# Attention products of an encoder step regrouped into fewer tiled stretches, with the chunk mask carried as contraction rows

## The chip, the core and the metric

The kernel runs on one core of a Trainium2 chip. TensorE (PE in the profile) multiplies, and its weight loads are listed apart as PEld; VectorE (DVE), ScalarE (ACT) and GpSimd (POOL) work on the results, and SyncE (SP) issues the transfers. The metric is the device time of one execution in microseconds (us), less is better.

## The reference

One step of a two-layer streaming encoder: 512 prompt frames of one new stream (positions 0 to 511) and 16 new frames of each of 8 running streams with 256 cached positions. Layer 0 mixes with forgetting attention (FoX, 16 heads of 64), layer 1 with latent attention (MLA, 16 heads of 64 + 32 rotary dimensions, mask by chunks of 64 frames); each is followed by cross attention over 256 memory rows (4 heads of 256) and a SwiGLU block of width 2816.

```
# fox
s = einsum('bqhd,bkhd->bhqk', q, k) * FOX_SCALE + cum_q - cum_k
p = softmax(where(k_pos <= q_pos, s, -inf)); o = einsum('bhqk,bkhd->bqhd', p, v)
o = (o * sigmoid(gate)) @ w_out
# mla
s = (einsum('bqhn,bkhn->bhqk', qn, k_nope) + einsum('bqhr,bkr->bhqk', qr, kr_all)) * MLA_SCALE
p = softmax(where(k_pos // 64 <= q_pos // 64, s, -inf)); o = einsum('bhqk,bkhd->bqhd', p, v)
# each layer
x = x + mixer(rmsnorm(x)); x = x + cross_attn(rmsnorm(x), mem_k, mem_v); x = x + swiglu(rmsnorm(x))
```

## The kernel before

The 512 prompt frames and the 128 frames of the running streams are five tiles of 128 rows. All stages follow one another on one core: FoX, cross attention 0, SwiGLU 0, MLA, cross attention 1, SwiGLU 1. Weights and activations are kept as two rounded parts (`hi`, `lo`), and a product is three passes of matmuls (`mm3`, `PASSES`, helper line L212; the big products go through `gemm`, L198). A product of plain float32 operands is recorded as two matmuls for each one that the program issues.

In the attention stages `merge` spreads three lists of steps evenly over each other: the prompt's attention for one pair of heads (or one head), the running streams' attention, and a list of big products for other heads (the `fill`). A scheduler then lays the instructions of each engine out in one fixed order, and may pull single instructions ahead of others that it expects to wait. TensorE works through that order.

Most matmuls use TensorE's whole array of 128 rows by 128 columns. Some address a part of it, because an operand has fewer rows or the result goes to a part of PSUM's 128 partitions. This text calls such a matmul *tiled*, and an unbroken series of matmuls of one tiling a *run*:

- FoX scores of the prompt (`scores`, L212): 64 contraction rows, head 0 of the pair in rows 0 to 63, head 1 in 64 to 127. Three passes for head 0 stand ahead of three for head 1, for each of four query tiles with 512, 384, 256 and 128 keys.
- FoX and MLA values of the prompt (`values`, L614 and L1587): 64 result columns for each of the two heads, once for each query tile.
- Running streams in FoX (L662, L687) and in cross attention (`scores` L903, `values` L928): four streams in four column strips of 32. In cross attention the two heads of a pair are two steps, each with keys or values loaded anew (`vr`, two buffers).
- MLA's chunk mask (L1561): a product of one row, `mrow` (-1e30 for the first 64 queries of a tile, else 0) times `mcol` (ones), added to the last 64 keys of every score tile behind its three passes of 96 rows.
- MLA running streams, rotary part of the scores (L1497): 32 rows (`KR` times `QR`), behind two products of 128 rows (L1495).

Of the kernel before, what the change touches and what calls it, by code (L numbers as in the profile page):

```python
# [18 lines left out]
P = 128  # L19
D = 1024  # L20
KD = D // P
NP = 512
# [33 lines left out]
C_END = 784  # L56


def const_table():
# [17 lines left out]
    return c  # L77


@with_exitstack  # L80
def fox_mla_kernel(ctx: ExitStack, tc: tile.TileContext, I, O):
# [22 lines left out]
    mrow = const.tile([1, P], BF16, name="mrow")  # L104
    G.memset(mrow, 0.0)
    G.memset(mrow[:, 0:64], NEG)
    mcol = const.tile([1, 64], BF16, name="mcol")
    G.memset(mcol, 1.0)

# [77 lines left out]
    def gemm(ops, n, done, parts=1):  # L187
        """One PSUM accumulation as a list of steps; ops() is asked for when the first step runs."""
# [56 lines left out]
    class Act:  # L245
        """A transposed activation in two tiles of four row blocks each."""
# [36 lines left out]
    def out_norm(out_tile, g_row, cls=None):  # L283
        """Runs the last output projection of a phase tile by tile, each tile's norm behind it."""
# [86 lines left out]
    # ---------------------------------------------------------------- FOX  # L371
    def fox_phase():
# [8 lines left out]
        with ExitStack() as st:  # L381
# [13 lines left out]
            def pt_tile():  # L395
                return fp.tile([P, NP], F32, tag="PT", name="PT", bufs=3)
# [164 lines left out]
            def prompt_list(pr):  # L561
# [10 lines left out]
                def scores(qt):  # L572
                    n = P * (qt + 1)
                    qs = slice(qt * P, (qt + 1) * P)
                    kT, qT = ks[pr][0], qs_[pr][0]
                    d["pw"] = []
                    for hh in range(2):
                        h = 2 * pr + hh
                        rs = slice(64 * hh, 64 * hh + 64)
                        pw = pw_tile()  # L580
                        G.tensor_scalar(pw[:, 0:n], d["ck"][hh][:, 0:n], -1.0, cq[:, qt, h:h + 1], ALU.mult, ALU.add)
                        G.affine_select(pw[:, n - P:n], pw[:, n - P:n], pattern=[[-1, P]], compare_op=ALU.is_ge,
                                        fill=NEG, base=0, channel_multiplier=1)
                        sp = psum_s()
                        mm3(sp[:, 0:n], [q[rs, qs] for q in qT], [k[rs, 0:n] for k in kT])
                        nm = small.tile([P, 1], F32, tag="nm", name="nm")
                        V.tensor_tensor_reduce(out=pw[:, 0:n], in0=sp[:, 0:n], in1=pw[:, 0:n], scale=-1.0,
                                               scalar=3.0e38, op0=ALU.add, op1=ALU.min, accum_out=nm)
                        ss = small.tile([P, 1], F32, tag="ssum", name="ssum")
                        A.activation(pw[:, 0:n], pw[:, 0:n], AF.Exp, scale=-1.0, bias=nm, accum_out=ss)  # L590
                        softmax_tail(pw, ss, n)
                        d["pw"].append(pw)

                def trans(qt):
                    n = P * (qt + 1)
                    d["PT"] = []
                    for hh in range(2):
                        pt = psum_t()
                        for kt in range(qt + 1):
                            T.transpose(out=pt[:, kt * P:(kt + 1) * P], in_=d["pw"][hh][:, kt * P:(kt + 1) * P],  # L600
                                        identity=ident)
                        PTt = pt_tile()
                        if hh == 0:
# [3 lines left out]
                        d["PT"].append(PTt)  # L607

                def values(qt):
                    qs = slice(qt * P, (qt + 1) * P)  # L610
                    op = psum_o()
                    for kt in range(qt + 1):
                        for hh in range(2):
                            T.matmul(op[64 * hh:64 * hh + 64, 0:P],  # L614
                                     lhsT=vs[g][:, kt, j * P + 64 * hh:j * P + 64 * hh + 64],
                                     rhs=d["PT"][hh][:, kt * P:(kt + 1) * P], start=(kt == 0), stop=(kt == qt))
                    V.tensor_tensor(sg[pr][:, qs], op[:, 0:P], sg[pr][:, qs], ALU.mult)

                L = [load]
                for qt in reversed(range(TT - 1)):  # L620
                    L += [lambda qt=qt: scores(qt), lambda qt=qt: trans(qt), lambda qt=qt: values(qt)]
                return L
# [149 lines left out]
    # ---------------------------------------------------------------- cross attention  # L772
    def cross_phase(l, nx, rest):
# [3 lines left out]
        with tc.tile_pool(name=f"x{l}", bufs=2, reuse_waits="tile") as xp:  # L777
# [99 lines left out]
            def sample_list(pr, bq):  # L877
# [3 lines left out]
                def keys(hh, b):  # L881
                    hc = slice((2 * pr + hh) * XD, (2 * pr + hh + 1) * XD)
                    if b % 2 == 0:
                        d["KT"][b // 2] = xp.tile([P, 2, 2, NMEM], F32, tag="KT", name="KT", bufs=2)
# [8 lines left out]
                    if b % 2 == 0:  # L893
                        V.tensor_copy(d["KT"][b // 2][:, 0], src)
                    else:
                        A.copy(d["KT"][b // 2][:, 1], src)

                def scores(hh):
                    if hh == 0:
                        d["sp"] = psum_s()  # L900
                    for dt in range(2):
                        for b in range(4):
                            T.matmul(d["sp"][32 * b:32 * b + 32, 0:NMEM], lhsT=Q[:, 2 * hh + dt, 4 * bq + b, :],  # L903
                                     rhs=d["KT"][b // 2][:, b % 2, dt, :], start=(hh == 0 and dt == 0),
                                     stop=(hh == 1 and dt == 1), tile_position=(0, 32 * b))
                    if hh == 1:
                        d["pw"] = xp.tile([P, NMEM], F32, tag="pws", name="pws", bufs=2)
                        softmax(d["pw"], d["sp"])
# [8 lines left out]
                def values(hh):  # L917
                    if hh == 0:
                        d["op"] = psum_o()
                    hc = slice((2 * pr + hh) * XD, (2 * pr + hh + 1) * XD)  # L920
                    vr = []
                    for b2 in range(2):
                        v = xp.tile([P, 4, XD], F32, tag="vr", name="vr", bufs=2)
                        S.dma_start(v, mv[:, 8 * bq + 4 * b2:8 * bq + 4 * b2 + 4, hc])
                        vr.append(v)
                    for mt in range(2):
                        for b in range(4):
# [770 lines left out]
```

## Time and profile before

| | |
|---|---|
| median of 3 runs | 2170.16 us (2169.56 to 2170.47) |
| span of the profiled execution, first to last instruction | 2169.7 us |
| TensorE matmul busy | 2116.0 us, 98% of the span |
| TensorE weight load busy | 1862.4 us, 86% |
| VectorE, ScalarE, GpSimd busy | 65%, 42%, 8% |
| granted TensorE clock, mean | 0.997 of full speed (2.4 GHz) |
| FoX attention 70 to 512 us; cross attention 0 577 to 710; MLA attention 1262 to 1515; cross attention 1 1580 to 1735 | of the span |

The profiled execution's own time is its span; no other figure of it is listed. Matmuls overlap, and a matmul's recorded duration reaches beyond the start of the next one, so the busy share says only that the engine hardly stood idle. What a matmul costs is read from the distance between starts.

### The profile page before, as it was taken

Reading aid. Unit: us, or ns where it says so; the run is one execution under the profiler, and the core shown is the slowest. Engines: PE = TensorE matmul, PEld = TensorE weight load, DVE = VectorE, ACT = ScalarE, POOL = GpSimd, SP = SyncE. Lnnn points to the kernel's source line nnn. Section 1 sums busy time; section 2 is a strip of 40 time slices with the busy share of each in tenths; the row PEclk is TensorE's granted clock in tenths of the full one; section 3 lists DMA queues with packets and bytes.
Section 4 is the critical chain, followed back from the end, with each engine's and each line's share of the span. In section 5 each row is a group of like instructions: output and inputs, shape, how many; then the busy total and the mean of one; then the engine's idle time right before and its main releaser. Section 6 shows DMA issues by size and latency. Waiting matters only on the chain. (4 is left out here: it accounts for less than half of the span.)

```text
span 2169.7 us, 36108 instructions
## 1 busy us (share of the span) xinstructions
PE 2116.0 (98%) x14253; PEld 1862.4 (86%) x14253; DVE 1404.2 (65%) x2719; ACT 904.0 (42%) x1809; POOL 178.7 (8%) x354
## 2 busy tenths in 40 slices
PE   7999999999999999999999999999999999999998
PEld 7888888888977799999999877777886799999997
DVE  5455555655446796687676566667545796786685
ACT  4444434554433453343334454544433443343342
POOL 1222121120000000000000200100100000000000
PEclk9999999999999999999999999999999999999999
DMA  8353443576354322222221320112435322322221
GB/s 235 112 145 107 127 124 116 178 231 211 108 178 143 117 78 79 87 88 78 78 78 53 109 72 26 51 40 60 154 129 190 94 84 78 98 75 82 78 88 59
DMA packets 279273, 234.34 MB, mean 108 GB/s; under 512 B 15664, under 2 KB 255920, under 8 KB 279104
## 3 DMA queue, kind: packets, MB, share of 16 engines
q1 hardware_dynamic: 279104, 232.03, 34.9%
q8 instruction: 113, 1.85, 0.4%
q14 instruction: 56, 0.46, 0.1%
HBM read 214.79 MB, written 17.21 MB: 107 GB/s over the span
## 5 line engine op out<-in xcount | busy, mean ns | idle before, releaser
L198 PE MATMUL mm<-hT,whi 128*128 128x320 f32 x1744 | 296.3, 314 | 3.3 <-ACT hT L216 3.3
L198 PEld LDWEIGHTS mm<-hT,whi 128*128 128x128 f32 x1744 | 261.1, 188 | 16.0 <-issue 9.8
L312 DVE TENSOR_TENSOR X<-mm,X 128x512 f32<-128x512 f32 x270 | 183.2, 687 | 127.5 <-PE mm L198 125.6
L145 DVE TENSOR_TENSOR wlo<-raw,whi 128x1024 fp32r<-128x1024 f32 (+4 forms) x145 | 169.7, 1175 | 105.8 <-ACT whi L144 69.8
L144 ACT CAST whi<-raw 128x1024 fp32r<-128x1024 f32 (+4 forms) x145 | 144.0, 1002 | 122.7 <-PE mm L198 75.6
L198 PE MATMUL mm<-whi,oT 128*128 128x512 f32 x544 | 185.2, 413 | 2.4 <-DVE X L312 2.1
L1069 ACT CAST whi<-tw 128x512 fp32r<-128x512 f32 (+1 forms) x120 | 91.9, 766 | 213.8 <-PE mm L198 127.5
L198 PE MATMUL mm<-whi,aT 128*128 128x512 f32 x560 | 173.0, 390 | 0.3 <-ACT aT L1034 0.3
L198 PE MATMUL mm<-hT,wlo 128*128 128x320 f32 x872 | 157.4, 313 | 0.0
L198 PEld LDWEIGHTS mm<-hT,wlo 128*128 128x128 f32 x872 | 133.7, 188 | 3.6 <-issue 3.5
L198 PE MATMUL mm<-whi,hT 128*128 128x256 f32 (+2 forms) x800 | 126.8, 297 | 1.9 <-ACT hT L216 1.0
L198 PE MATMUL mm<-s,whi 128*128 128x320 f32 x768 | 128.2, 309 | 0.0
L226 POOL TENSOR_SCALAR rstd<-ss 128x1 f32<-128x1 f32 x49 | 16.7, 340 | 1306.2 <-ACT hn L224 1302.1
L198 PEld LDWEIGHTS mm<-whi,aT 128*128 128x128 f32 x560 | 104.4, 188 | 22.5 <-ACT aT L1034 1.2
L198 PEld LDWEIGHTS mm<-whi,oT 128*128 128x128 f32 x544 | 98.0, 190 | 26.1 <-issue 5.7
L198 PEld LDWEIGHTS mm<-s,whi 128*128 128x128 f32 x768 | 116.6, 188 | 0.0
L198 PEld LDWEIGHTS mm<-whi,hT 128*128 128x128 f32 x800 | 109.5, 192 | 7.8 <-issue 3.2
L1070 DVE TENSOR_TENSOR wlo<-tw,whi 128x512 fp32r<-128x512 f32 (+1 forms) x120 | 103.4, 862 | 19.0 <-ACT whi L1069 18.3
L198 PE MATMUL mm<-wlo,oT 128*128 128x512 f32 x272 | 109.9, 406 | 0.0
L198 PE MATMUL mm<-wlo,aT 128*128 128x512 f32 x280 | 108.8, 389 | 0.0
L212 PE MATMUL ps_s<-kT,qT 128*128 128x256 f32 (+8 forms) x576 | 102.5, 329 | 0.2 <-ACT qs L1503 0.2
L1069 ACT CAST whi<-raw 128x1024 fp32r<-128x1024 f32 x44 | 46.3, 1052 | 131.7 <-PE mm L198 71.4
(337 smaller groups left out, 4342.6 us busy)
## 6 DMA issues: line engine op xcount, KB each, us to landing
rawg<-w_ffn_gu SPq DMA_DIRECT2D x80, 512.0 KB, 3.8
raw<-w_ffn_down SPq DMA_DIRECT2D x44, 512.0 KB, 3.6
raw<-w_x_kv SPq DMA_DIRECT2D x32, 512.0 KB, 4.8
kr<-cache_mem_k SPq DMA_DIRECT2D x64, 256.0 KB, 4.2
vr<-cache_mem_v SPq DMA_DIRECT2D x32, 512.0 KB, 4.6
raw<-w_fox_in SPq DMA_DIRECT2D x30, 512.0 KB, 4.3
kr<-cache_fox_k SPq DMA_DIRECT2D x16, 512.0 KB, 5.5
vr<-cache_fox_v SPq DMA_DIRECT2D x16, 512.0 KB, 3.9
```

Of the source, the lines that this page charges most:

```text
L144: A.copy(hi[:, 0:m], raw[:, 0:m])
L145: V.tensor_tensor(lo[:, 0:m], raw[:, 0:m], hi[:, 0:m].bitcast(F32), ALU.subtract)
L198: T.matmul(st["ps"][:, 0:n], lhsT=l, rhs=r, start=(j == 0), stop=(j == m - 1))
L212: T.matmul(out, lhsT=la[li], rhs=ra[ri], start=start and i == 0, stop=stop and i == 2)
L226: G.tensor_scalar(r, ss, EPS, None, ALU.add)
L312: V.tensor_tensor(xs, ps, xs, ALU.add)
L1069: A.copy(hi[:, o:o + m], src)
L1070: V.tensor_tensor(lo[:, o:o + m], src, hi[:, o:o + m].bitcast(F32), ALU.subtract)
```

## The change

Five edits, here with the line numbers of the changed kernel where they matter:

1. FoX prompt: `scores` takes a list of query tiles; tiles 1 and 0 share one step, and within a pass the matmuls alternate between the two heads. `values` takes two query tiles into one PSUM bank and one multiplication. The order of steps becomes scores 3, transposes 3, scores 2, transposes 2, values of 3 and 2, scores of 1 and 0, their transposes, their values.
2. MLA prompt: `values` likewise by two query tiles.
3. MLA mask: keys and queries get four more contraction rows (100 instead of 96), filled once from a small table; the one-row product, `mrow` and `mcol` are gone. Row t is 1 for the keys of chunk 2t+1 and -1e30 for the queries of chunk 2t.
4. MLA running streams: `KR` and `QR` are 128 rows, zero beyond row 31, cleared once.
5. Cross attention of the running streams: keys of both heads first (`KT`, four buffers), then `load_v` with all four value tiles (`vr`, four buffers), one `scores` and one `values` step for both heads.

The pool `PT` grows from three to five buffers; the scratch for software-made descriptors shrinks (no transfer uses it).

```diff
@@ FoX prompt_list
-                def scores(qt):
...
-                        sp = psum_s()
-                        mm3(sp[:, 0:n], [q[rs, qs] for q in qT], [k[rs, 0:n] for k in kT])
...
+                def scores(qts):
...
+                    for qt in qts:
+                        n, qs = P * (qt + 1), slice(qt * P, (qt + 1) * P)
+                        for i, (li, ri) in enumerate(PASSES):
+                            for hh in range(2):
+                                T.matmul(sps[hh][:, at[qt]], lhsT=qT[li][rows[hh], qs], rhs=kT[ri][rows[hh], 0:n],
+                                         start=(i == 0), stop=(i == 2))
...
+                def values(q2):
                     op = psum_o()
+                    for i in range(2):
+                        qt = 2 * q2 + i
+                        for kt in range(qt + 1):
+                            for hh in range(2):
+                                T.matmul(op[64 * hh:64 * hh + 64, i * P:(i + 1) * P],
...
+                    V.tensor_tensor(sg[pr][:, qs], op[:, 0:256], sg[pr][:, qs], ALU.mult)
...
+                return [load, lambda: scores([3]), lambda: trans([3]), lambda: scores([2]), lambda: trans([2]),
+                        lambda: values(1), lambda: scores([1, 0]), lambda: trans([1, 0]), lambda: values(0)]
@@ cross_phase sample_list
-                L = []
-                for hh in range(2):
-                    L += [lambda hh=hh, b=b: keys(hh, b) for b in range(4)] + [lambda hh=hh: scores(hh)]
-                return L + [trans, lambda: values(0), lambda: values(1), turn]
+                return [lambda hh=hh, b=b: keys(hh, b) for hh in range(2) for b in range(4)] + \
+                    [load_v, scores, trans, values, turn]
@@ mla_phase
+            KRs = [mp.tile([P, KS], F32, name=f"KR{i}") for i in range(2)]
...
+            QKM = QKD + MROWS
...
+            msk = mp.tile([QKM, 2 * NP], F32, tag="qrow", name="msk")
+            S.dma_start(msk[MROW:QKM], I["masks"])
+            for src, tiles in ((msk[MROW:QKM, 0:NP], [h for p_ in kTs for h in p_]), (msk[MROW:QKM, NP:2 * NP], qTs)):
+                for hi, lo in tiles:
+                    A.copy(hi[MROW:QKM], src)
+                    G.memset(lo[MROW:QKM].bitcast(F32), 0.0)
+            for k in KRs:
+                G.memset(k, 0.0)
...
-                L = [lambda: G.memset(PZ, 0.0)]
+                def zeros():
+                    G.memset(QR, 0.0)
+                    G.memset(PZ, 0.0)
...
-                        mm3(sp[:, 0:n], [q[:, qs] for q in heads[pr, hh]], [k[:, 0:n] for k in kTs[j][hh]], stop=False)
-                        T.matmul(sp[:, n - 64:n], lhsT=mrow, rhs=mcol, start=False, stop=True)
+                        mm3(sp[:, 0:n], [q[:, qs] for q in heads[pr, hh]], [k[:, 0:n] for k in kTs[j][hh]])
...
-                for qt in reversed(range(TT - 1)):
-                    L += [lambda qt=qt: scores(qt), lambda qt=qt: trans(qt), lambda qt=qt: values(qt)]
+                for q2 in (1, 0):
+                    for qt in (2 * q2 + 1, 2 * q2):
+                        L += [lambda qt=qt: scores(qt), lambda qt=qt: trans(qt)]
+                    L.append(lambda q2=q2: values(q2))
```

How TensorE's order moves is shown at two places, and ScalarE's at one. The number of matmuls in a row stands behind its x.

TensorE before, third list of the running streams in cross attention 0 (L903 and L928 are the tiled scores and values, L890 transposes keys, L212 the prompt's scores and values, L198 the output projection):

```order
L890 MATMUL ps_t<-cst,kr 128x128 x4
L212 MATMUL ps_o<-PT_8103,v_8018 128x256
L903 MATMUL ps_s<-KT,Qp_6909 32x256
L890 MATMUL ps_t<-cst,kr 128x128 x4
...
L890 MATMUL ps_t<-cst,kr 128x128 x4
L903 MATMUL ps_s<-KT,Qp_6909 32x256 x2
L198 MATMUL mm<-whi,oT_7257 128x512
L198 MATMUL mm<-whi,oT_7258 128x512
L198 MATMUL mm<-wlo,oT_7257 128x512
L903 MATMUL ps_s<-KT,Qp_6909 32x256 x5
```

The same list after the change (L926 are the scores of both heads, L952 the values of both):

```order
L204 MATMUL mm<-whi,oT_7132 128x512
L926 MATMUL ps_s<-KT,Qp_6792 32x256 x16
L204 MATMUL mm<-wlo,oT_7131 128x512
...
L935 MATMUL ps_t<-cst,pws 128x128 x2
L882 MATMUL ps_t<-cst,hn 128x128 x4
L952 MATMUL ps_o<-vr,PTs 32x256 x16
```

Before, the second head's eight matmuls stood in pieces of 1, 2 and 5 with whole-array work between; after, sixteen stand together, and so do the values.

TensorE before, MLA attention, the last query tile of a pair of heads (L212 the three score passes of a head, L1561 the mask):

```order
L212 MATMUL ps_s<-kT_13100,qT_13985 128x128
L212 MATMUL ps_s<-kT_13101,qT_13985 128x128
L212 MATMUL ps_s<-kT_13100,qT_13986 128x128
L1561 LDWEIGHTS mrow
L1561 MATMUL ps_s<-mcol,mrow 128x64
L212 MATMUL ps_s<-kT_13102,qT_14008 128x128
L212 MATMUL ps_s<-kT_13103,qT_14008 128x128
L212 MATMUL ps_s<-kT_13102,qT_14009 128x128
L1561 LDWEIGHTS mrow
L1561 MATMUL ps_s<-mcol,mrow 128x64
```

And after the change, the passes of a head at a like place (L218), with L1624 the values:

```order
L218 MATMUL ps_s<-kT_12991,qT_12999 128x256
L218 MATMUL ps_s<-kT_12992,qT_12999 128x256
L218 MATMUL ps_s<-kT_12991,qT_13000 128x256
L204 MATMUL mm<-wlo,ckT_12977 128x256 x2
L1624 MATMUL ps_o<-PT,vsb 64x128 x5
```

The 64 mask products and their weight loads are gone, and nothing tiled stands between the passes any more.

ScalarE after the change, start of the MLA stage (L230 the last norm, L1270 the mask rows of the eight key and query tiles, L1340 the evacuation of the first down projection, which stood right behind L230 before):

```order
L230 ACTIVATE hn,ss<-X 128x1024
L1270 CAST kT_12985<-msk 4x512
L1270 CAST kT_12987<-msk 4x512
L1270 CAST kT_12989<-msk 4x512
L1270 CAST kT_12991<-msk 4x512
L1270 CAST qT_12993<-msk 4x512
L1270 CAST qT_12995<-msk 4x512
L1270 CAST qT_12997<-msk 4x512
L1270 CAST qT_12999<-msk 4x512
L1340 COPY qrow<-mm 128x336 x2
```

Eight casts now stand ahead of that evacuation on ScalarE.

## Rows read from the trace of the kernel before

**Rows 1.** The page, its first part: busy time, share of the span, instructions.
```profile
PE 2116.0 (98%) x14253; PEld 1862.4 (86%) x14253; DVE 1404.2 (65%) x2719; ACT 904.0 (42%) x1809; POOL 178.7 (8%) x354
```

**Rows 2.** Busy time by stretch (FoX, cross 0, MLA): length, engines, clock, DMA share, GB/s.
```profile
70.00:512.00 442.00, 439.34 (x3665) 385.06 (x3664) 246.34 (x650) 201.10 (x441) 90.48 (x167) 1.00 0.49 147
...
577.00:710.00 133.00, 126.65 (x935) 100.48 (x933) 71.17 (x142) 49.53 (x113) 0.00 (x0) 0.99 0.48 155
...
1262.00:1515.00 253.00, 251.87 (x1633) 190.62 (x1634) 168.47 (x441) 124.85 (x349) 21.17 (x49) 1.00 0.15 44
```

**Rows 3.** What TensorE waited for: us in total, times, longest us.
```profile
PE ps_t L890 <- DMA kr<-cache_mem_k: 7.3, 11, 2.1
PE ps_o L928 <- DMA vr<-cache_mem_v: 6.1, 4, 1.9
```

**Rows 4.** Timeline of TensorE in FoX: start us, us, engine, line, names, shapes, count.
```profile
251.78 1.34 PE L198 MATMUL mm<-hT,wlo 128*128 128x320 f32 x8
253.05 0.66 PE L614 MATMUL ps_o<-PT,vsb 128*64 128x128 f32 x8
253.63 1.43 PE L198 MATMUL mm<-hT,whi 128*128 128x320 f32 x8
255.00 0.67 PE L662 MATMUL ps_s<-KT,Qbd 128*32 128x272 f32 x8
```

**Rows 5.** The same view in SwiGLU 0, where nothing is tiled.
```profile
747.26 1.34 PE L198 MATMUL ps_s<-hT,wlo 128*128 128x320 f32 x8
748.43 2.51 PE L198 MATMUL mm<-hT,whi 128*128 128x320 f32 x16
```

**Rows 6.** The same view in FoX, a values run of twice the size.
```profile
78.74 1.09 PE L614 MATMUL ps_o<-PT,vsb 128*64 128x128 f32 x16
```

**Rows 7.** The same view in MLA, the mask of one head.
```profile
1307.76 0.62 PE L212 MATMUL ps_s<-kT,qT 96*128 96x256 f32 x3
1308.31 0.20 PE L1561 MATMUL ps_s<-mcol,mrow 1*128 1x64 bf16 x1
1308.44 0.71 PE L1521 MATMUL ps_o<-PT,H 128*128 128x128 f32 x4
```

**Rows 8.** The same view in FoX, prompt scores of 512 keys and plain products behind them.
```profile
118.48 0.97 PE L212 MATMUL ps_s<-kT,qT 64*128 64x512 f32 x6
119.39 1.21 PE L198 MATMUL mm<-whi,hT 128*128 128x256 f32 x8
120.44 0.64 PE L198 MATMUL mm<-wlo,hT 128*128 128x256 f32 x4
120.91 0.28 PE L198 MATMUL mm<-whi,hT 128*128 128x256 f32 x1
```

**Rows 9.** The same view in MLA, the running streams' scores.
```profile
1376.43 1.08 PE L1495 MATMUL ps_s<-CT,H 128*128 128x272 f32 x4
1377.44 0.72 PE L1497 MATMUL ps_s<-KR,H 32*128 32x272 f32 x2
1378.09 0.44 PE L198 MATMUL mm<-wlo,cqT 128*128 128x384 f32 x1
```

**Rows 10.** The same view in cross attention 0, the running streams' scores of the fourth list.
```profile
691.86 1.07 PE L903 MATMUL ps_s<-KT,Qp 128*32 128x256 f32 x16
...
694.56 0.62 PE L903 MATMUL ps_s<-KT,Qp 128*32 128x256 f32 x2
...
697.44 0.63 PE L903 MATMUL ps_s<-KT,Qp 128*32 128x256 f32 x4
...
698.88 1.05 PE L903 MATMUL ps_s<-KT,Qp 128*32 128x256 f32 x10
```

**Rows 11.** Timeline of ScalarE at the start of MLA, with idle time and its releaser.
```profile
1180.97 0.44 ACT L1308 COPY qrow<-mm 128x336 f32<-128x336 f32 x1 [3.66 <-PE mm L198]
...
1224.45 0.58 ACT L216 CAST kT<-ps_t 32x512 fp32r<-32x512 f32 x1 [1.41 <-PE ps_t L1295]
```

**Rows 12.** Timeline of GpSimd at the start of MLA.
```profile
1215.60 0.31 POOL L1460 MEMSET H<- 128x256 f32 x1
```

More of the change, by code (lines that the diff above doesn't have):

```diff
@@ L77, in const_table, with mask_table @@
     return c
+def mask_table():
+    n = np.arange(NP)
+    m = np.zeros((MROWS, 2 * NP), np.float32)
+    for t in range(MROWS):
+        m[t, 0:NP] = (n // 64) == 2 * t + 1
+        m[t, NP:] = np.where((n // 64) == 2 * t, NEG, 0.0)
+    return m
 @with_exitstack
@@ L395, in pt_tile @@
             def pt_tile():
[L396 removed]
+                return fp.tile([P, NP], F32, tag="PT", name="PT", bufs=5)
             def logf_list():
@@ L570, in load @@
                         d["ck"].append(cb)
-                def scores(qt):
-                    n = P * (qt + 1)
-                    qs = slice(qt * P, (qt + 1) * P)
+                def scores(qts):
                     kT, qT = ks[pr][0], qs_[pr][0]
-                    d["pw"] = []
+                    rows = [slice(64 * hh, 64 * hh + 64) for hh in range(2)]
+                    sps, pws, at, o = [], [], {}, 0
+                    for qt in qts:
+                        at[qt] = slice(o, o + P * (qt + 1))
+                        o += P * (qt + 1)
@@ new lines, in scores @@
+                        pws.append(pw)
+                        sps.append(psum_s())
+                    for qt in qts:
+                        n, qs = P * (qt + 1), slice(qt * P, (qt + 1) * P)
[4 more added lines that the diff above has]
+                    for hh in range(2):
+                        for qt in qts:
+                            c = at[qt]
+                            pw, sp = pws[hh][:, c], sps[hh][:, c]
+                            nm = small.tile([P, 1], F32, tag="nm", name="nm")
+                            V.tensor_tensor_reduce(out=pw, in0=sp, in1=pw, scale=-1.0,
+                                                   scalar=3.0e38, op0=ALU.add, op1=ALU.min, accum_out=nm)
+                            ss = small.tile([P, 1], F32, tag="ssum", name="ssum")
+                            A.activation(pw, pw, AF.Exp, scale=-1.0, bias=nm, accum_out=ss)
+                            softmax_tail(pw, ss, P * (qt + 1))
@@ L893, in keys, with scores @@
                     if b % 2 == 0:
-                        V.tensor_copy(d["KT"][b // 2][:, 0], src)
+                        V.tensor_copy(d["KT"][hh, b // 2][:, 0], src)
                     else:
[L896 to L908, printed above, removed]
+                        A.copy(d["KT"][hh, b // 2][:, 1], src)
+                def scores():
+                    sp = psum_s()
+                    for hh in range(2):
+                        for dt in range(2):
+                            for b in range(4):
+                                T.matmul(sp[32 * b:32 * b + 32, 0:NMEM], lhsT=Q[:, 2 * hh + dt, 4 * bq + b, :],
+                                         rhs=d["KT"][hh, b // 2][:, b % 2, dt, :], start=(hh == 0 and dt == 0),
+                                         stop=(hh == 1 and dt == 1), tile_position=(0, 32 * b))
+                    d["pw"] = xp.tile([P, NMEM], F32, tag="pws", name="pws", bufs=2)
+                    softmax(d["pw"], sp)
                 def trans():
@@ L1397, in q_T @@
                 def q_T(hh):
-                    tl = [mp.tile([QKD, NP], F32R, tag=f"qT{i}", name=f"qT{i}", bufs=4) for i in range(2)]
+                    tl = qTs[(2 * pr + hh) % 4]
                     pt = psum_t()
```

138 lines of the change are left out of this document (65 added, 73 removed).

## The prediction

> **What bounds the kernel now.** I read the page's busy shares first, then busy time by stretch, then TensorE's waits, then its timeline inside the attention stages. The page has matmuls under way for 98% of the span [rows 1]. In the FoX, first cross-attention and MLA stretches TensorE is idle for 442 - 439.3 = 2.7, 133 - 126.7 = 6.3 and 253 - 251.9 = 1.1 us, while VectorE, the next engine, is busy for 56, 54 and 67% [rows 2]; the clock is at its upper level of 2.4 GHz (granted 0.99 to 1.00). So the stream of matmuls sets the time, and the list of its waits explains little; in cross attention two transfers hold it, for 7.3 us (`kr`) and 6.1 us (`vr`) over both phases [rows 3]. What the busy share hides is how far apart matmuls start. In SwiGLU, without a tiled run, eight matmuls of 320 columns take 748.43 - 747.26 = 1.17 us, 0.146 each [rows 5]. The same eight in FoX take 253.05 - 251.78 = 1.27 ahead of a tiled run and 255.00 - 253.63 = 1.37 between two [rows 4]. That difference is what the change goes for.
>
> **The price of one run.** Take the values run at 253.05 [rows 4]. Entry: 1.27 - 1.17 = 0.10 us. Body: 253.63 - 253.05 = 0.58 us for four pairs of matmuls (eight records; the two heads lie side by side). A run of sixteen records spans 1.09 us against 0.66 [rows 4, 6], so a pair costs 0.43 / 4 = 0.11, four 0.44, and 0.14 of the body is neither. Behind the run, 1.37 - 1.17 = 0.20, of which 0.10 is the next run's entry and 0.10 the first weight load that nothing covers. Together 0.10 + 0.14 + 0.10 = 0.34 us, whatever the run holds. So joining two runs saves about 0.34, and splitting one costs it.
>
> I counted runs through both emitted orders, from start to end: 301 before, 152 after. Of the 149 that go, 64 are masks, 16 `KR` products, 16 MLA values (42 to 26), 15 FoX values (34 to 19), 4 FoX scores (35 to 31), 16 cross scores and 16 cross values (24 to 8 each), and 2 in MLA's preparation.
>
> **Masks.** The three passes of a head start at 1307.76 and the work behind its mask at 1308.44: 0.68 us [rows 7]. A plain 256-column matmul takes (120.91 - 120.44) / 4 = 0.118 [rows 8], three 0.35. One mask thus costs 0.33 us, though its matmul has 64 columns; 64 cost 20.9. Its replacement, four more contraction rows, costs nothing: the 0.118 and 0.146 are those of matmuls with all 128 rows, and 100 rows can't need more.
>
> **`KR`.** Four records of 128 rows take 1377.44 - 1376.43 = 1.01 us, with an entry of 0.10 in it: 0.23 each. The two of 32 rows take 0.65 [rows 9]. At 128 rows they would take 0.46, and entry and reload go: 0.19 + 0.10 + 0.10 = 0.39 in nine cases. In seven a values run follows directly and one border stays, about 0.29. Sum 5.5. The zeros written into them are costed below.
>
> **Values and prompt scores.** 31 joined values runs at 0.34: 10.5. Row-tiled scores: the run of 512 keys takes 119.39 - 118.48 = 0.91 us for three passes of both heads; at 2.4 GHz 512 columns last 0.213, three 0.64; 0.27 is over, and entry (0.10) and reload (119.39 to 120.44 is 1.05, less eight at 0.118: 0.11) bring it to 0.48 [rows 8]. Four times between that and 0.34: 1.7. The two runs in MLA's preparation: 0.8.
>
> *Alternating the heads* I cost at zero. The six matmuls of that run need 6 x 0.213 = 1.28 us one after another and took 0.91 with everything, so the heads already ran side by side though one is issued behind the other. The Trainium skill, page "TensorE: Matmul & The Clock Gate", section "Part 3: Packing small matmuls — row/col tiling", says otherwise: matmuls start and end strictly in program order. By that rule the old order would run the heads in turn, and the new one would save three passes for each query tile. The row speaks against it, and I go by the row.
>
> **Cross attention.** In lists three and four of each phase, the second head's scores are cut into three pieces. One list shows 0.62 + 0.63 + 1.05 = 2.30 us for pieces of 2, 4 and 10 records against 1.07 for a whole run of 16 [rows 10]. The pieces overlap what follows by about 0.08 each (0.66 against 0.58 in [rows 4]), so 1.23 - 0.16 = 1.07 is lost in them, because a piece of one or two streams fills one or two of four column strips, and two more entries and reloads cost 0.40. Four such cuts: 5.9. The values of one head are cut in 2 and 6 in all eight lists; a piece of four records costs 0.63 - 0.08 + 0.20 = 0.75, eight 6.0. Joining the two heads saves 16 times an entry, a reload and the 0.11 by which a run of four groups (1.07 - 0.08) exceeds four at (1.07 - 0.63) / 2 = 0.22: 0.31, or 5.0. Sum 16.9.
>
> The value tiles are loaded a step ahead of the scores into four buffers instead of behind the first head's values into two. What waited for them, 6.1 us, I take as gone (bounds 0 and 6.1).
>
> **What it adds.** At the start of MLA eight casts of 512 columns stand on ScalarE ahead of the first evacuation. A cast of that width from 32 rows takes 0.58 us [rows 11], eight 4.6. The cover is the 3.66 us that ScalarE idles there [rows 11]; up to 1.0 is late, and then the evacuations and transposed activations queued behind it are what TensorE waits for. On GpSimd, clearing `QR` is eight times as wide as the clear that took 0.31 [rows 12]: between 0.3 and 2.5, I take 2, ahead of the last norm of the down projection; the order has moved another tile's products in front of the transposes that need it, so at most 2 is exposed. Eight small clears and two of `KR` lie in a stretch where GpSimd only serves norms. `kr` loads are asked for sooner and stay one queue; I add 1 us to their 7.3, and 1 for waits inside joined runs. Together 5 (bounds 0 and 15).
>
> **The sum.** 20.9 + 5.5 + 10.5 + 1.7 + 0.8 + 16.9 = 56.3 us of matmul stream, 6.1 of waits, less 5: 57.4. The profiled execution's span is 2169.7, 0.5 below the median of the runs, so 2170.2 - 57.4 = 2112.8; I say 2113.
>
> **Rivals.**
> *The time comes back as waits.* MLA loses some 31 of 253 us, the orders are fixed, and what TensorE found ready there it may now find late: scores wait for softmax, transposes for its scaling, values for the copies. If half of the 56.3 returns: 2141. For it: TensorE has hardly any idle time to show that slack is large. Against it: VectorE would rise from 67% to 168.5 / 222 = 76% in MLA [rows 2], far from a bound.
> *Joining saves little.* If a run's cost belonged to its operands (weights of another shape, another bank) and not to its borders, only what is deleted pays: 20.9 + 5.5 + 6.1 - 5 = 27.5, 2143. Against it: entry and reload are measured on the untiled neighbours [rows 4].
> *More than forecast.* If the heads did run in turn in places, alternating saves 3 x (512 + 384 + 256 + 128) columns at 2.4 GHz = 1.6 us for each of eight pairs, 13: 2100. The 0.91 us speaks against it. The rule of the Trainium skill named above would make it so.
> *Slower: the transfer queue of cross attention.* SP issues in order. A `vr` load of the next list waits for this list's values, and `kr` loads stand behind it. There are 64 `kr` loads; if each held TensorE for the longest wait seen, 2.1 us [rows 3], 134 would be lost: 2170 + 134 - 57 = 2247. It decides from 0.9 us for each load (57.4 / 64). Against it: with four buffers a load waits for work one list back.
>
> **Chances.** Forecast 75%, waits 10%, little from joining 5%, more 5%, slower 3%, all given back 2%. The forecast's own spread: the price of a run between 0.29 and 0.39 is 7 us either way, the waits 0 to 15 and the `vr` term 0 to 6, so 2101 to 2127. The range reaches towards the first two rivals without taking them in: 2101 to 2131. This kernel's runs lie within 0.9 us, so 0.2% (4.3 us) is about what a measurement tells from no change. Faster 94%, same 2%, slower 4%.
>
> **What the changed profile would show.** No L1561 rows; the FoX stretch about 7 us shorter, MLA some 30, each cross phase 8 to 12; `KR` records 0.23 apart behind L1495; cross scores and values in runs of 32 records near 2 us; no `vr` wait; ScalarE's casts at the MLA start ending before its first evacuation is late. I would be wrong if the passes of 100 rows started further apart than those of 96, if a joined run took as long as its parts, or if TensorE's waits in MLA or cross attention grew by tens of microseconds.

## The result, and the profile after

The changed kernel took 2134.31 us (median of 4 runs, 2123.33 to 2136.22) beside 2169.95 for the kernel before (4 runs): a ratio of 0.9831, 95% interval 0.9807 to 0.9856. It is faster by 1.7%, by 36 us where 57 were forecast, and the median lies 3 us outside the range. The profiled execution is the longest of the four, with a span of 2134.4.

The first part of the changed kernel's page answers to [rows 1]:

```profile
PE 2071.8 (97%) x14189; PEld 1863.8 (87%) x14189; DVE 1394.1 (65%) x2695; ACT 900.2 (42%) x1793; POOL 176.0 (8%) x362
```

Next, busy time by stage, with stages cut at the same instructions in both kernels: FoX attention, cross attention 0 up to SwiGLU, MLA attention, cross attention 1, SwiGLU 1. The columns are as in [rows 2]; a row's length less its PE time is TensorE's idle time. The kernel before:

```profile
70.30:511.10 440.80, 438.14 (x3655) 383.87 (x3653) 245.62 (x646) 200.59 (x439) 90.48 (x167) 1.00 0.49 146
576.90:744.80 167.90, 159.94 (x1105) 127.35 (x1103) 95.18 (x176) 62.39 (x136) 3.17 (x8) 0.99 0.46 145
1229.50:1514.10 284.60, 281.69 (x1816) 213.65 (x1814) 188.83 (x480) 140.87 (x384) 24.87 (x57) 1.00 0.18 53
1514.10:1731.20 217.10, 205.42 (x1395) 169.20 (x1391) 125.32 (x216) 84.97 (x175) 10.25 (x20) 1.00 0.46 145
1731.20:2159.70 428.50, 426.90 (x2548) 400.01 (x2548) 321.03 (x513) 162.69 (x251) 7.15 (x10) 1.00 0.26 78
```

The changed kernel:

```profile
72.70:512.70 440.00, 433.11 (x3657) 384.57 (x3655) 241.27 (x623) 196.11 (x431) 83.14 (x167) 1.00 0.49 147
576.40:736.10 159.70, 152.27 (x1106) 128.18 (x1104) 93.71 (x176) 62.01 (x136) 3.16 (x8) 0.99 0.46 146
1221.90:1484.80 262.90, 254.88 (x1754) 210.67 (x1751) 187.65 (x483) 139.27 (x370) 23.30 (x56) 1.00 0.19 59
1484.80:1694.50 209.70, 199.58 (x1394) 170.44 (x1390) 122.86 (x216) 83.77 (x174) 8.90 (x20) 0.99 0.47 148
1694.50:2124.50 430.00, 428.43 (x2548) 401.53 (x2548) 321.15 (x512) 162.53 (x251) 7.13 (x10) 1.00 0.26 78
```

MLA gives 21.7 us, the cross phases 8.2 and 7.4, FoX only 0.8, and SwiGLU 1, which nobody touched, loses 1.5. TensorE's idle time in FoX and MLA grows from 2.7 and 2.9 to 6.9 and 8.0, although the stages are shorter. The list of its waits names new ones; of [rows 3], the `vr` row is gone and `kr` has grown from 7.3 to 9.8:

```profile
PE ps_t L913 <- DMA kr<-cache_mem_k: 9.8, 11, 2.3
...
PE mm L204 <- ACT whi L150: 5.0, 5, 2.1
...
PE ps_s L685 <- DVE nm L607: 2.8, 2, 2.5
PE ps_t L1609 <- DVE hn L331: 1.8, 4, 0.5
...
PE ps_s L218 <- ACT qs L1539: 1.2, 3, 0.9
```

The matmul stream itself is what was forecast. TensorE's timeline in cross attention, a list's scores and values, answers to [rows 10]:

```profile
628.25 1.93 PE L926 MATMUL ps_s<-KT,Qp 128*32 128x256 f32 x32
630.11 1.00 PE L204 MATMUL mm<-hT,wlo 128*128 128x320 f32 x5
...
633.99 1.93 PE L952 MATMUL ps_o<-vr,PTs 128*32 128x256 f32 x32
635.85 0.56 PE L204 MATMUL mm<-hT,whi 128*128 128x320 f32 x2
```

A list's 32 records lie in one run of 1.93 us, where the four runs of [rows 10] lasted 3.37 together. The same view in MLA answers to [rows 9]:

```profile
1425.81 0.62 PE L1533 MATMUL ps_s<-KR,H 128*128 128x272 f32 x2
1426.07 0.83 PE L204 MATMUL mm<-whi,ckT 128*128 128x256 f32 x4
```

`KR` with 128 rows takes 0.26 us to the next start, with 32 rows 0.65.

To see all of it I summed both traces. The cost of a tiled run is the distance from the last whole-array matmul ahead of it to the second one behind it, less those two's usual steps and less recorded idle time. By that sum the masks cost 20.0 us before and nothing after, `KR` gives 6.6, cross scores and values go from 52.5 to 33.9, values of FoX and MLA from 62.0 to 52.4, FoX scores from 29.3 to 28.2. With what small items add and take it is 56 us of stream. Against it stand 9.1 us more idle time (44.0 to 53.1 in all), 7.0 more in steps that are longer than usual for their shape without recorded idle time (short stalls from here on), and 4.6 more in stretches of half clock (granted clock 0.50, see the last section): 56 - 21 = 35, the difference of the spans. The 4.6 are of this execution: its trace has four such stretches, that of the kernel before two, and the second profile below one.

### The profile page after: what moved, and what is told of

Its sections match the earlier page's. It is cut to its first block, busy times and chain, and to the rows that moved or that the text cites. A ratio compares the mean times of both kernels' runs of the same rounds, so it can differ in the third digit from the quotient of the medians.

```text
span 2134.4 us, 35883 instructions
## 1 busy us (share of the span) xinstructions
PE 2071.8 (97%) x14189; PEld 1863.8 (87%) x14189; DVE 1394.1 (65%) x2695; ACT 900.2 (42%) x1793; POOL 176.0 (8%) x362
## 5 line engine op out<-in xcount | busy, mean ns | idle before, releaser
L204 PEld LDWEIGHTS mm<-hT,whi 128*128 128x128 f32 x1744 | 262.6, 189 | 12.0 <-ACT hT L222 5.7
L204 PEld LDWEIGHTS mm<-whi,hT 128*128 128x128 f32 x800 | 110.0, 193 | 10.3 <-ACT whi L150 4.5
L204 PE MATMUL ps_s<-whi,aT 128*128 128x512 f32 x320 | 98.6, 389 | 0.0
```

The lines of the kernel that those rows point to most:

```text
L204: T.matmul(st["ps"][:, 0:n], lhsT=l, rhs=r, start=(j == 0), stop=(j == m - 1))
```

## The experiments

Each kernel was timed beside the kernel before on the same chip; ratios are to that, with 95% intervals. Lengths of stages are those of the views above, cut at the same instructions.

**Is the loss always there?** The changed kernel again.

> The changed kernel, unaltered. Theory A: the shorter matmul stream came as priced (some 55 us), and about 20 us came back as idle time, short stalls and half-clock intervals that the new order brings with it. Then the median stays at 2130 to 2136, and a second profile shows the same idle places (ScalarE's casts at the MLA start, about 2 us; VectorE's score sums in FoX, about 2.5 us; kr loads). Rival B: the first execution met a disturbance, and the usual time is that of the fastest execution, 2123; then most executions lie at 2121 to 2126 and those idle places are gone.

Measured: 2128.77 (2125.59 to 2132.77) beside 2166.89; 0.9824 (0.9810 to 0.9838). The ratio is the first one again. The median lies 1.2 us below theory A's range and 2.8 above rival B's, on a chip on which the kernel before is 3.1 faster too. Another profile has FoX at 438.7, the cross phases at 156.8 and 212.3, MLA at 262.6, 51.0 us idle and short stalls of the same size. For MLA theory A holds: the stage repeats within 0.3 us, so its loss belongs to the order. The 2 us for `whi` at the MLA start came and went; in the first profile ScalarE waits there 4.04 us for a weight's transfer, in the second 2.46, and in neither behind the casts. SwiGLU 1 is back at 428.4: the 1.6 us there were a stretch of half clock.

**One edit at a time.** Of the five edits in the section on the change, `mask_only` has the third alone, `cross_only` the fifth, `fox_only` the first, `mlaval_only` the second, and `mla_only` the second to fourth; all else is the kernel before, but for the smaller scratch.

> The kernel before with the mask as four contraction rows and nothing else. The emitted order loses 64 mask runs and gains 4 values runs. Price of 0.33 us for a mask and 0.34 for a run: -21 + 1.4, and 2 for the wait at the MLA start: 2152. If the loss in the MLA stage belongs to this edit (softmax and transposes found late), half comes back: 2160. If nothing comes back and the casts hide: 2149.

> The kernel before with the cross-attention regrouping and nothing else (24 runs to 8, scores and values each, over both phases). Price by run borders and cut pieces as forecast: -16.9, vr waits gone -6.1, kr waits up by 2 to 3: 2150. Rival, joining saves little and only the vr waits go: 2164. Rival, kr loads stand behind vr loads on the issuing engine: over 2170.

> The kernel before with the FoX regrouping and nothing else (34 values runs to 19). Price of runs in full: -15 x 0.34 - 1.7 = -6.8: 2163. Theory A: two query tiles per step hold their PSUM and their softmax longer, the running streams' scores wait for VectorE, and 3 to 6 us come back: 2167 to 2170. Rival, joining saves nothing and the waits stay: 2173.

> The kernel before with MLA's values by two query tiles and nothing else (42 runs to 27 in the emitted order, the masks stay). Price of a run in full: 15 x 0.34 = 5.1: 2162. Half back as waits: 2164.5. Joining saves nothing: 2167.

> The kernel before with all three MLA edits (mask rows, values by two query tiles, KR on 128 rows), FoX and cross attention as before. Stream by the trace of the full change: masks 20 + KR 6.6 + values 5.5, some 32 us. Theory A: a third comes back inside the stage, which was 21.7 us shorter in the full change: 2145. Rival B: the shortfall came from the edits ahead of and behind it: 2136.

| kernel | us, beside before | ratio (interval) | its stage, before to this |
|---|---|---|---|
| mask_only | 2156.55, 2166.89 | 0.9956 (0.9943 to 0.9968) | MLA 284.6 to 274.8 |
| cross_only | 2154.70, 2166.89 | 0.9943 (0.9930 to 0.9955) | cross 385.0 to 364.0 |
| fox_only | 2166.20, 2166.89 | 0.9991 (0.9981 to 1.0000) | FoX 440.8 to 438.4 |
| mlaval_only | 2166.31, 2169.52 | 0.9985 (0.9977 to 0.9994) | MLA 284.6 to 281.1, half clock in it |
| mla_only | 2142.89, 2169.52 | 0.9877 (0.9864 to 0.9891) | MLA 284.6 to 262.9 |

Stages from the view of busy time, first `mla_only`, then the two phases of `cross_only`:

```profile
1229.60:1492.50 262.90, 255.01 (x1753) 210.80 (x1751) 187.53 (x483) 139.50 (x370) 23.38 (x56) 1.00 0.20 59
...
577.80:735.50 157.70, 150.99 (x1106) 126.71 (x1104) 93.71 (x176) 61.76 (x136) 3.16 (x8) 1.00 0.47 148
...
1507.20:1713.50 206.30, 198.93 (x1396) 170.74 (x1394) 124.27 (x217) 84.93 (x175) 9.40 (x20) 0.99 0.48 152
```

Against the kernel before beside them, `mask_only` gains 10.3 us, the case of half coming back (10); `mlaval_only` 3.2, between half (2.5) and full (5); `fox_only` 0.7, which its interval does not tell from nothing, and `mla_only` 26.6, each as its theory A had it; `cross_only` 12.2, where 20 were expected and 6 by its rival.

The MLA and FoX edits fall short in their own stages, and `mla_only` has exactly the MLA stage of the full change: what happens there comes neither from FoX nor from cross attention. In its pair of profiles `cross_only` shortens the two phases by 21.0, just what was forecast, but one pair misleads here. In seven profiles with the old cross attention the two phases together take 377.7 to 385.0 (mean 381.6), in three with the new one 364.0 to 369.4 (mean 367.5): 14.1 apart.

The edits of the three stages add up as far as this can tell: alone they are worth 0.0123, 0.0057 and 0.0009 of the time, 0.0189 together, and the full change 0.0169 and 0.0176. Inside MLA that is open, since `KR` was not run alone. The mask edit alone moves other work: it shortens MLA by 9.8 us, and 2.1 of what is missing go to the values, which the scheduler then cuts into 46 runs (42 before); with the values joined it doesn't.

**Is it the rows?** `mask_gone` drops the one-row product and puts nothing in its place, so its prompt attends to all keys in MLA and its result is another one; `rows_kept` adds the rows and keeps the product.

```diff
 # mask_gone
-    mm3(sp[:, 0:n], [q[:, qs] for q in heads[pr, hh]], [k[:, 0:n] for k in kTs[j][hh]], stop=False)
-    T.matmul(sp[:, n - 64:n], lhsT=mrow, rhs=mcol, start=False, stop=True)
+    mm3(sp[:, 0:n], [q[:, qs] for q in heads[pr, hh]], [k[:, 0:n] for k in kTs[j][hh]])
 # rows_kept: those two lines stay, and
+            QKM = QKD + MROWS
...
+                    A.copy(hi[MROW:QKM], src)
+                    G.memset(lo[MROW:QKM].bitcast(F32), 0.0)
```

> The kernel before without the chunk mask: the one-row products are left out and nothing stands in their place, so the prompt's MLA attends to all keys. No mask rows, no casts, no clears. The emitted order loses 64 mask runs and gains 4 values runs, 18 us of matmul stream. Theory A: about half of that comes back because a denser stream in MLA meets softmax, copies and PSUM that are not ready: 2156, as with the four rows. Rival B: what came back there is the price of the four rows (longer passes, casts ahead of ScalarE's work): 2148.

> The kernel before with the four contraction rows added and the one-row products kept, so the mask is applied twice. Theory A: rows, casts and clears cost 0 to 2 us: 2167 to 2169. Rival B: they cost what was missing in the run with the mask alone, 8 to 10 us: 2175 to 2177.

Measured: 2162.11 and 2168.76 beside 2169.52; 0.9968 (0.9956 to 0.9981) and 0.9995 (0.9984 to 1.0006). The MLA stage of `mask_gone` by the view of busy time:

```profile
1228.30:1504.40 276.10, 268.59 (x1754) 208.41 (x1754) 188.88 (x481) 140.57 (x385) 25.43 (x57) 1.00 0.19 58
```

276.1 without any mask work, 274.8 with the rows, and 7.5 us idle where before there were 2.9. `mask_gone` gains 7.4 us, even less than the 14 of its theory A, and rival B's 22 are out. The time of `rows_kept` is that of the kernel before within 1.3 us either way (its MLA stage reads 287.4, with 6.83 us of half clock in it). So the rows, casts and clears cost nothing that can be measured; it is the missing work that uncovers waits.

**Whose waits in MLA?** In that stage I listed every step between whole-array matmuls (those of `KR` left out) that, with its idle time, was over 0.08 us longer than usual for its shape: 54 steps and 5.7 us before, 89 and 14.6 in the second profile of the changed kernel. Two kinds carry most of the growth: score passes (10 with 0.8 us, now 22 with 4.4; before, those next to a mask run don't enter the list) and transposes of probabilities (5 with 0.7, now 11 with 3.3). Each score tile takes one PSUM bank of its pool until softmax has read it. `three_s` gives the scores three banks and the big products two; `late_trans` puts the transposes one step later.

```diff
 # three_s
-    pmm = ctx.enter_context(tc.tile_pool(name="pmm", bufs=3, space=PSUM))
+    pmm = ctx.enter_context(tc.tile_pool(name="pmm", bufs=2, space=PSUM))
-        return pat.tile([P, 512], F32, tag="s", name="ps_s", bufs=2)
+        return pat.tile([P, 512], F32, tag="s", name="ps_s", bufs=3)
 # late_trans
-    for qt in (2 * q2 + 1, 2 * q2):
-        L += [lambda qt=qt: scores(qt), lambda qt=qt: trans(qt)]
+    two = (2 * q2 + 1, 2 * q2)
+    L += [lambda qt=qt: scores(qt) for qt in two] + [lambda qt=qt: trans(qt) for qt in two]
```

> The changed kernel with three PSUM banks for scores and two, not three, for the big products. Theory A: the waits that came back in MLA and FoX are for a score bank that softmax has not yet left (in MLA 22 stalls of score passes, 4.5 us with their short ones, against 0.8 before; in FoX 1.7 to 2.8 us for the running streams' scores): they go to about 1, and MLA falls from 262.8 by 3 to 5 us. What two banks cost the big products shows in the SwiGLU stages, which share their banks otherwise. Rival B: score banks are not what is late, MLA stays at 262 to 263.

> The changed kernel with MLA's prompt in the order scores of two query tiles, then their transposes, then their values. Theory A: transposes of the probabilities come too soon behind the softmax (11 stalls, 3.3 us, against 0.7 before); with one step more between them they go to 1, MLA falls by 2. Rival B: the score passes, now one behind the other, wait longer for their banks and for the two buffers of probabilities, and MLA grows by 2 to 6.

Measured: 2144.46 and 2134.34 beside 2168.17; 0.9880 (0.9860 to 0.9900) and 0.9840 (0.9822 to 0.9858). `three_s`, MLA and SwiGLU 1:

```profile
1228.40:1484.50 256.10, 251.46 (x1749) 208.88 (x1746) 183.75 (x479) 138.06 (x369) 24.53 (x56) 1.00 0.20 61
...
1700.10:2133.10 433.00, 428.48 (x2548) 399.62 (x2548) 322.20 (x514) 162.60 (x251) 6.97 (x9) 1.00 0.26 79
```

MLA falls by 6.8, more than the 3 to 5 of theory A; SwiGLU 1 pays 4.6, and the kernel is slower than the changed one. FoX, where the same bank was to help, doesn't shorten (441.5), though the bank that its products lost is in that figure. Later transposes only move the wait: that of the transposes (`hn` L331) falls from 1.8 to 0.3 us, the running streams' scores (L1531) wait 2.2 that the changed kernel doesn't have, and MLA takes 264.5. That is on the side of rival B, below its 2 to 6 us, and the time is that of the changed kernel.

**Why is `kr` late?** SyncE's own waits in the changed kernel have this row (us in total, times, longest):

```profile
SPq L909 <- PE ps_t L962: 10.7, 6, 1.8
```

`kr` loads wait there for the transposes of `osb`, the gathered result of the list before, which takes one of the four buffers of the `kr` ring (buffers used in turn: a load waits until the last reader of its buffer is done). The kernel before has the same row, and a longer one, in the trace that the prediction was read from; there L886 loads `kr` and L939 transposes `osb`:

```profile
SPq L886 <- PE ps_t L939: 16.1, 6, 4.3
```

In the changed kernel, SyncE's timeline at the longest wait of cross attention 0, and TensorE's:

```profile
635.51 0.50 SPq L909 DMA_DIRECT2D kr<-cache_mem_k  x1
636.11 0.93 SPq L850 DMA_DIRECT2D kr<-kvd  x2
638.83 0.37 SPq L909 DMA_DIRECT2D kr<-cache_mem_k  x1
```

```profile
638.16 0.60 PE L962 MATMUL ps_t<-cst,osb 128*128 128x128 f32 x4
...
644.52 1.09 PE L913 MATMUL ps_t<-cst,kr 128*128 128x128 f32 x4 [2.31 <-DMA kr<-cache_mem_k]
```

The second load of the list goes out at 638.83, behind the `osb` transposes at 638.16, and TensorE has its data at 644.52. `osb_own` gives `osb` a buffer of its own, `before_osb` does so in the kernel before.

```diff
-    d["osb"] = xp.tile([P, 512], F32, tag="kr", name="osb", bufs=4)
+    d["osb"] = xp.tile([P, 512], F32, tag="osb", name="osb", bufs=1)
```

> The changed kernel with the gathered result of a cross-attention list (osb) in a buffer of its own instead of one of the four kr buffers. Theory A: TensorE's waits for kr (9.8 and 11.3 us in two profiles) come from the ring: the kr load at the head of a list is issued only when the osb transposes have given a buffer back, and lands 4 us later. Then they fall to 3 to 6 us and the time by 4 to 8 against the changed kernel, 42 to 46 below before. Rival B: the transfers' rate sets them, and the time stays 36 to 38 below before.

> The kernel before with osb in a buffer of its own and nothing else. Theory A: the buffer that osb holds became the limit through the new order, which asks for eight kr tiles in a row; before, other steps stood between and the vr loads were as late, so the gain is 0 to 4 us. Rival B: the ring was the limit all along, and the gain is the 9 to 11 us that it brought the changed kernel.

Measured: 2119.62 beside 2168.17, 0.9776 (0.9755 to 0.9796); and 2159.83 beside 2169.04, 0.9957 (0.9945 to 0.9969). The cross phases of `osb_own`, and its wait for `kr`:

```profile
573.40:726.70 153.30, 149.81 (x1107) 127.14 (x1105) 93.53 (x176) 61.91 (x136) 3.16 (x8) 1.00 0.48 152
...
1474.20:1677.00 202.80, 197.18 (x1394) 169.31 (x1391) 122.78 (x215) 83.74 (x174) 9.76 (x20) 1.00 0.49 153
```

```profile
PE ps_t L913 <- DMA kr<-cache_mem_k: 1.6, 2, 1.1
```

Those of `before_osb`, and the only wait for a transfer of the memory that is left there:

```profile
575.90:737.60 161.70, 157.59 (x1107) 126.41 (x1105) 94.71 (x176) 62.04 (x136) 3.16 (x8) 1.00 0.48 151
...
1506.50:1718.00 211.50, 204.53 (x1395) 168.80 (x1393) 124.84 (x216) 84.69 (x175) 9.41 (x20) 1.00 0.48 149
```

```profile
PE ps_o L928 <- DMA vr<-cache_mem_v: 4.6, 5, 1.3
```

Of my theory one half stands: it is the ring and not the rate that cost this time. `osb_own` is 48.6 us below the kernel before, more than the 42 to 46 expected. The wait is not always gone, though: three later kernels with the same buffer show 3.2, 3.2 and 6.1 us of it. The other half fell: the slot held the kernel before as much, 9 us there (6.7 to 11.9 by the interval) against some 11 in the changed kernel (0.9776 against 0.9824 and 0.9831, on other chips, so to some 5 us). With the ring free on both sides, the regrouping of cross attention brings 373.2 - 356.1 = 17.1 us, by one profile on each side; the three later kernels, with the cross attention of `osb_own`, take 357.6, 357.0 and 362.9, the last with a stretch of half clock in it.

**Banks and heads, on top of `osb_own`.** `osb_bank` lends every third prompt score tile of MLA a bank of the products' ring; `osb_seq` puts FoX's heads one behind the other again; `osb_mla3` moves one bank from products to scores (prompt and running streams) for the MLA pairs alone.

```diff
 # osb_bank
-    sp = psum_s()
+    alt[0] = (alt[0] + 1) % 3
+    sp = psum_s() if alt[0] else pmm.tile([P, 512], F32, tag="mm", name="ps_s")
 # osb_seq
-    for i, (li, ri) in enumerate(PASSES):
-        for hh in range(2):
+    for hh in range(2):
+        for i, (li, ri) in enumerate(PASSES):
 # osb_mla3, psum_s; psum_mm gives the products two banks there
+    mx[2] = (mx[2] + 1) % 3
+    if mx[0] and mx[2] == 0:
+        return pmm.tile([P, 512], F32, tag="mx", name="ps_s", bufs=1)
```

> The changed kernel with osb in a buffer of its own and, in MLA alone, every third score tile of the prompt in a bank of the big products' ring. Theory A: what MLA got back as waits is mostly for a score bank; the stage falls from 263 to 256 to 259 as with three banks everywhere, the other stages stay, and the time is 3 to 6 below that of the kernel with osb alone, some 52 to 55 below before. Rival B: the big products of MLA, short of a bank now and then, wait as much: no difference, 48 to 49 below before.

> The changed kernel with osb in a buffer of its own and, in FoX, the three score passes of one head ahead of those of the other, not alternating. Theory A: the heads run side by side in either order, so FoX stays within 1.5 us of 438.7, a little less if the first head's bank is left sooner. Rival B, heads issued one behind the other run in turn: FoX 13 us longer.

> The changed kernel with osb in a buffer of its own and, from the first pair of heads of MLA to the last and there alone, one PSUM bank moved from the big products (two left) to the scores of prompt and running streams (three). Theory A: the waits that came back in MLA are for score banks; the stage falls from 263 to 256 or 257, as it did with three banks everywhere, all other stages stay, and the time is 54 to 56 below before. Rival B: that gain came from the order that two product banks gave, not from the third score bank, or is lost to the products: MLA at 261 or more, the time 46 to 50 below before.

Measured: 2121.24 and 2122.51 beside 2169.04, 0.9778 (0.9765 to 0.9792) and 0.9782 (0.9769 to 0.9794); `osb_mla3` 2114.30 beside 2168.20, 0.9746 (0.9726 to 0.9766), the lowest of all, though its interval overlaps that of `osb_own`. Its MLA stage, that of `osb_bank`, and that of `osb_own` to compare:

```profile
1215.00:1470.90 255.90, 250.79 (x1748) 208.70 (x1746) 184.07 (x482) 138.77 (x370) 24.68 (x56) 1.00 0.20 61
```

```profile
1213.80:1478.70 264.90, 254.60 (x1753) 211.74 (x1752) 185.35 (x482) 138.13 (x369) 24.15 (x56) 0.99 0.19 57
```

```profile
1211.10:1474.20 263.10, 255.06 (x1753) 210.83 (x1751) 187.56 (x483) 139.40 (x370) 23.25 (x56) 1.00 0.19 59
```

A third score bank for both users shortens MLA by 7.2 us and idles 5.1 instead of 8.0; the stalls of score passes go from 4.5 to 1.8. The emitted order differs too: the values stand in 21 runs instead of 26, worth some 2 of the 7.2 us, so the bank isn't cleanly parted from the order. A bank lent to the prompt alone brings nothing (264.9, of which 2 are a stretch of half clock), although that order has 21 such runs as well. `osb_seq` has FoX at 439.1 against 438.7, where its rival had 13 us more: the order of the heads is worth nothing.

## Why the prediction came out as it did

**The price of a run and the stream were right.** 56.3 us were priced and 56 measured. By part: masks 20.9 forecast, 20.0 measured; `KR` 5.5 and 6.6; MLA's values, 16 runs at 0.34, 5.4 and 5.5; cross attention 16.9 and 18.6. FoX was priced too high: its 15 values runs gave 4.1 (0.27 each), its scores 1.1 of 1.7, and the running streams' runs lost some 0.4. That the totals agree this closely is partly luck, since FoX's excess cancels what `KR` and cross attention gave beyond their price.

**The step that failed is the sum of waits:** "6.1 of waits, less 5", 1.1 us in favour. Measured on the two profiles, idle time, short stalls and half clock took 20.7. With the `vr` waits gone as forecast, what the change added is thus some 27 us, where 5 were set down with 15 as the upper bound. In the second profile half clock adds nothing, and idle time is still 7.0 above that of the kernel before. The range hid part of this: its lower end, 2101, is the sum of its bounds (7 and 5), its upper one, 2127, is not; the same sum there (7, 10 and 6) gives 2136. By place:

- *MLA*, 29.6 us forecast (32.6 of stream less 3), 21.7 measured. What I added up there, casts, clears and the rows' cost, is nothing (`rows_kept`; the eight casts end in time, MLA's preparation is 0.5 us shorter). What I left to a rival, scores and transposes waiting for softmax, is 10 us, also in `mla_only` and without rows in `mask_gone`. I had argued that VectorE is far from a bound at 76%; it is at 187.65 / 262.9 = 71% and the waits came all the same. That share did not tell what a chain through two score banks does; with a third bank the stage is 6.8 and 7.2 us shorter (`three_s`, `osb_mla3`).
- *Cross attention*, 21.0 forecast (16.9 + 6.1 - 2), 15.6 measured, 14.1 by the means above. The `vr` waits are gone as forecast, yet idle time fell only from 19.6 to 17.6 us, since `kr` waits took their place, and short stalls grew by 2.3. By the same view, seven profiles with the old cross attention idle 16.9 us there in the mean, three with the new one (two of the changed kernel, `cross_only`) 16.8. The prediction looked for the `kr` queue behind `vr`; the queue that mattered was the ring that `kr` shares with `osb`.
- *FoX*, 6.8 forecast, 0.8 measured, 2.1 and 2.4 in two other profiles of the same order; the means of eight profiles with the old order and seven with the new (`three_s` and `osb_seq` left out) are 2.3 apart (441.4 and 439.1). Of what is missing, 2 are from the price, the rest idle time. At 427 us VectorE's score sums stand behind the splitting of a weight that is late, and both score banks stay full. Its timeline, with idle time in brackets, and TensorE's row:

```profile
425.62 1.23 DVE L151 TENSOR_TENSOR wlo<-raw,whi 128x1024 fp32r<-128x1024 f32 x1 [1.51 <-ACT whi L150]
426.77 0.42 DVE L607 CUSTOM_DVE_ANT_0 pw<-ps_s,pw 128x256 f32<-128x256 f32 x1
```

```profile
427.46 0.67 PE L685 MATMUL ps_s<-KT,Qbd 128*32 128x272 f32 x8 [2.51 <-DVE nm L607]
```

  A step that fills both banks at once leaves the running streams' scores none. No experiment takes this apart (`three_s`, with a bank less for the products, brought FoX nothing), so that cause is argued, not shown.

**The rivals.** "The time comes back as waits" was priced as half of the stream, 2141, and given one chance in ten; about a third came back. "Joining saves little" is refuted by the sums of runs. "More than forecast": the heads ran side by side before, as `osb_seq` confirms; in the run of [rows 8] the six matmuls start in three pairs 0.01 us apart, though all three of one head are issued ahead of the other's. The rule of the Trainium skill that spoke for it (page "TensorE: Matmul & The Clock Gate", section "Part 3: Packing small matmuls — row/col tiling") does not hold for these two heads: 439.1 and 438.7 us for the two orders. "Slower by the transfer queue" did not come. That `osb_mla3` (2114.30) comes out at the forecast is chance: 9 us of it are the ring's, which the kernel before lost too.

**What stays open:** the rest of FoX's idle time, how much of MLA's 7.2 us is the bank and how much the order that came with it, the idle time that is left in MLA with three banks (5.1 against 2.9), what `KR` brings alone, and why `kr` still waits up to 6.1 us with the ring free.

## What to carry to other kernels

When a change thins the stream of the engine that sets the time, forecast what comes back from the rings through which that stream passes (here two score banks and four load buffers), not from the busy shares of the other engines: a third of the gain came back with no engine near its bound. Look at who else holds a slot of a ring before pricing a wait as gone: a result parked in a load ring cost 9 us before the change and 11 after, and where one wait for a load was removed the next took its place. An edit measured alone can move other work: without the one-row products the scheduler cut the values into 46 runs instead of 42. And one pair of profiles can flatter an edit: the cross phases read 21.0 us shorter in one pair and 14.1 in the means of several.

## What was not expected of the hardware

Stretches of half clock, 3.41 us long each (two profiles have one of twice that). In the changed kernel's trace the granted clock is 0.50, the 1.2 GHz level, behind two pauses of TensorE at the head of SwiGLU 1 (1.63 us, and 1.47 us up to 1704.15); the columns are those of the stages:

```profile
1705.95:1709.36 3.41, 3.41 (x15) 3.41 (x14) 3.41 (x4) 0.08 (x1) 0.00 (x0) 0.50 0.02 8
1694.50:1705.95 11.45, 9.90 (x67) 9.24 (x68) 10.69 (x13) 5.81 (x10) 1.48 (x2) 1.00 0.50 146
```

One costs 1.6 us: SwiGLU 1 with its three product banks takes 428.4 or 428.5 in twelve profiles without and 429.9 or 430.0 in four with one. The same pauses were followed by none in the second profile of the changed kernel (428.4), so a pause alone doesn't decide it. Profiles had none to four of them ahead of the last 10 us. They go with much of the spread of the kernel before, whose runs lay within 0.9 us on the first chip and between 2162.29 and 2171.19 on another (15 runs): the two at a mean clock of 0.995 took 2168.91 and 2171.19, the one at 0.999 2162.94. They are not all of it: four runs at 0.996 lie between 2166.91 and 2170.50. What the prediction called the reach of a measurement, 0.2%, was too fine for single runs and right for medians.
